# A two-layer encoder in split fp32: layer norm's PSUM bank, the first and last microseconds, the bank order of the matmuls, and inputs laid out feature-major by the host

## The chip, the cores and the metric

The kernel runs on one core of one Trainium2 chip. The metric is the device time of one execution in microseconds; lower is better. Every program shown was run several times and the median is given. A separate profiled execution gives the trace from which durations are read.

## What is computed

Two encoder layers of width 2048 over 256 tokens, with a second sequence of 256 memory tokens:

```python
def reference(x, mem, ...):
    for layer in range(2):
        h = rms_norm(x, norm_mix_g[layer])
        if layer == 0:   # conformer convolution (GLU, depthwise conv 31, layer norm, silu) beside differential attention
            x = x + mixer_conv_diff(h, ab_w_in, ..., ab_w_out)
        else:            # S5 state space, GELU, gated projection
            x = x + mixer_s5(h, ..., s5_w_val, s5_w_gate)
        x = x + memory_cross_attention(rms_norm(x, norm_xa_g[layer]), rms_norm(mem, norm_mem_g[layer]),
                                       xa_wq[layer], xa_wk[layer], xa_wv[layer], xa_wo[layer])
        x = x + conv_ffn(rms_norm(x, norm_ffn_g[layer]), ffn_w_up[layer], ffn_dw[layer], ffn_db[layer], ffn_w_down[layer])
    return rms_norm(x, final_g)
```

Everything is fp32. Nearly all the work lies in the linear layers: a [256 x 2048] activation times weights of 2048 columns and more, 5632 x 2 columns in the feed-forward (`ffn_w_up`) and back (`ffn_w_down`).

## The kernel before

**Split products.** A product of fp32 precision is made of three matmuls: weights and activations are each split into a rounded part `hi` (type fp32r) and a remainder `lo`; hi·hi, hi·lo and lo·hi are added up in PSUM. `wtile` loads 512 KB of weights into one of four `raw` buffers (queue of SP), ScalarE (ACT) casts `hi` from it (L209), VectorE (DVE) subtracts `lo` (L211); `hi` and `lo` have three buffers each.

**Two forms of the linear layer.** `lin_ws` holds weights stationary and gives the output feature-major. Per 128 rows of the contraction and for each half `c` of 256 output columns it issues one matmul of 256 columns ("low", L253: `lo` weights, `hi` activations) and one of 512 ("both", L250: `hi` weights, both parts of the activations). The halves `c` lie in two PSUM banks; a call has 64 such matmuls, 16 for each `wtile`. `lin_xs` holds activations stationary and gives the output token-major: for each 128 rows six matmuls of 512 columns, three for each token block `tb`, and the token blocks lie in two banks (L287; with `tail`, the second block's matmuls of the last weight tiles wait until the first block's are issued, L290). The accumulators of both forms come from a pool `acc` of two buffers of two banks; small PSUM tiles come from `pst`, two tags `ps` and `pt` of two banks each, taken in turn.

**Activations.** `transpose_chunk` turns 512 features of a token-major tile with 8 TensorE transposes (L156) against `ident` and evicts them as `hi` (ACT, L163) and `lo` (DVE, L164), scaled by the norm's gain. It serves the residual `X` and the memory tokens alike; the per-token factor of the norm is applied after the linear layers.

**Order.** Instructions of each engine run in the order that a scheduler of the framework sets from a simulated timeline. Beside the main line of code run generators (`self.side`): after each weight tile `background` plays some of their steps. `conv_ln` is one, with the depthwise convolution and layer norm of the conformer branch: sums over channels by matmuls with a matrix of ones into a tile `ps_mu` (mean, L518), squares `sq` (ACT, L523), sums of these into a second tile `ps_var` (L527), then `rsqrt_steps` (shift and subtract, then three Newton iterations of four DVE operations, L115 to L118), the scaling (L532), Silu (L537) and the split into `ao` (L299, L300). `ao` is the second half of the operand of the output projection `ab_w_out`; the first half, `bo`, comes from the eight attention heads, whose last step is the transpose `ps_oT` (L476).

**Memory tokens.** `mem_T(0)` stands ahead of the attention heads, `mem_T(1)` ahead of the second half of layer 0's down projection. Both transpose the memory tokens.

**Ends.** The start loads X in four chunks on SP's queue between the weight tiles of the first `lin_ws`, and small constants on POOL's queue. The end is the last down projection of layer 1 (n = 3, `tail=3`) into one accumulator, then per token block: add to X (L694), sum of squares (L696), product with the final gain (L697), the reciprocal root on one column, the scaling of four slices (L706, L708) and four output DMAs (L709).

Of the kernel before, what the change touches and what calls it, by code (L numbers as in the profile page):

```python
# [34 lines left out]
class Build:  # L35
# [43 lines left out]
    def setup(self):  # L79
# [3 lines left out]
        nc.sync.dma_start(self.X[:, :, 0:512], a["x"][0])  # L83
        nc.sync.dma_start(self.ident, a["ident"])
# [24 lines left out]
    def rsqrt_steps(self, out, v, i32, t, cost):  # L109
        nc = self.nc  # L110
        nc.vector.tensor_scalar(i32, v.bitcast(I32), 1, None, op0=ALU.logical_shift_right)
        nc.vector.tensor_scalar(i32, i32, -1, 0x5F3759DF, op0=ALU.mult, op1=ALU.add)
        y = i32.bitcast(F32)
        for it in range(3):
            nc.vector.tensor_tensor(t, y, y, op=ALU.mult)  # L115
            nc.vector.tensor_tensor(t, t, v, op=ALU.mult)
            nc.vector.tensor_scalar(t, t, -0.5, 1.5, op0=ALU.mult, op1=ALU.add)
            nc.vector.tensor_tensor(out if it == 2 else y, y, t, op=ALU.mult)  # L118
            yield cost
# [46 lines left out]

    def xslice(self, n):
# [32 lines left out]
    def wtile(self, src):  # L200
# [3 lines left out]
        dma = nc.sync.dma_start(raw, src)  # L204
# [32 lines left out]
    def lin_ws(self, w, xt):  # L237
# [5 lines left out]
        for k4 in range(4):  # L243
            hi, lo = self.wtile(w[k4])
            for kk in range(4):
                xh, _, x2 = xt(k4 * 4 + kk)
                first, last = k4 + kk == 0, k4 + kk == 6
                for c in range(2):
                    sl = slice(c * 128, c * 128 + 128)
                    both = lambda: nc.tensor.matmul(ps[:, c], lhsT=hi[:, kk, sl], rhs=x2, start=first, stop=last)  # L250
                    if first:
                        both()
                    nc.tensor.matmul(ps[:, c, 1], lhsT=lo[:, kk, sl], rhs=xh, start=False, stop=False)  # L253
                    if not first:
                        both()
# [7 lines left out]
    def lin_xs(self, w, xt, kts, ps=None, stop=True, tail=0):  # L263
# [3 lines left out]
        start = ps is None  # L267
        if start:
# [4 lines left out]
        for k2 in range(nk // KD):  # L273
            hi, lo = self.wtile(w[k2])
            for kk in range(KD):
# [3 lines left out]
                for tb in range(2):  # L279
                    sl = slice(tb * 128, tb * 128 + 128)  # L280
                    ops = [(xh, hi, first, False), (xh, lo, False, False), (xl, hi, False, last)]
                    for x, y, st, sp in ops:
# [20 lines left out]
    def mem_T(self, layer):  # L303
# [7 lines left out]
        for n in range(4):  # L311
            m = []
            for tb in range(2):
                if layer == 0:
                    m.append(mm[:, tb, n * 512 : n * 512 + 512])
                else:
                    t = self.M.tile([128, 512], F32, tag="c0", name="mst", bufs=2)
                    nc.sync.dma_start(t, a["mem"][n, :, tb])
                    m.append(t)
            if layer == 0:  # L320
                self.sumsq(m, n)
            self.mT.append(self.transpose_chunk(m, n, 6 + layer))
# [26 lines left out]
    def mixer0(self):  # L349
# [5 lines left out]
        nc.gpsimd.dma_start(cdw, a["conv_dw"])  # L355
        cv = M.tile([128, 3, 8], F32, name="cv")
        nc.gpsimd.dma_start(cv, a["conv_v"])
        nabs = M.tile([128, 2, NTOK], F32, name="nabs")
        nc.gpsimd.dma_start(nabs, a["nabs"])
        lq = M.tile([128, 4, 64], F32, name="lq")  # L360
        nc.gpsimd.dma_start(lq, a["diff_l"].partition_broadcast(128))
        sub_g = M.tile([128, 1], F32, name="sub_g")
        nc.gpsimd.dma_start(sub_g, a["subln_g"])


        lp = M.tile([128, 2, 64], F32, name="lp")
        le = M.tile([128, 2], F32, name="le")
        lam = M.tile([128, 1], F32, name="lam")
        nc.vector.tensor_tensor(lp, lq[:, 0::2, :], lq[:, 1::2, :], op=ALU.mult)
        nc.vector.tensor_reduce(le, lp, axis=AX.X, op=ALU.add)  # L370
        nc.scalar.activation(le, le, AF.Exp)
# [873 lines left out]
```

## Time and profile before

| | |
|---|---|
| runs | 2931.55, 2935.66, 2938.13 us; median 2935.66 |
| profiled execution | 2932.71 us, span 2930.9 us, mean granted TensorE clock 0.994 |
| TensorE (PE) busy | 2881.2 us, 98% of the span, 16769 matmuls |
| DVE busy | 2213.4 us, 76% |
| ACT busy | 1493.2 us, 51% |
| DMA | 674.16 MB, mean 230 GB/s |

The busy time of PE counts matmuls with modelled ends that overlap the next one, so the distance from start to start tells how fast a stream runs. Groups of instructions are named by the line of the kernel that issues them; `x128` is a count, the next numbers are busy time and the mean of one instruction in ns, and behind the bar stands the idle time of the engine just before them. A window row gives for each engine the busy time in that stretch, then the granted clock, the mean busy share of the DMA engines, and GB/s.

### The profile page before, as it was taken

What the parts mean: (1) busy time and instruction counts of PE and PEld (TensorE: products, weight loads), DVE (VectorE), ACT (ScalarE), POOL (GpSimd) and SP (SyncE); (2) the same over time, 40 slices, a digit from 0 to 9 for tenths busy, and PEclk for the clock granted to TensorE, in tenths of its full rate; (3) what the DMA queues carried; (4) which work ended last, traced back from release to release, by engine and by line L of the source; (5) the groups of instructions that cost most, each with busy time, mean ns of one, the idle gap of its engine ahead of it and who ended that gap; (6) DMA issues with size and microseconds to landing.
All of it is one profiled execution on the core that took longest, in us unless ns stands there. A gap on an engine that the chain in (4) does not pass through costs nothing. (4 is left out here: it accounts for less than half of the span.)

```text
span 2930.9 us, 44468 instructions
## 1 busy us (share of the span) xinstructions
PE 2881.2 (98%) x16769; PEld 2436.5 (83%) x16769; DVE 2213.4 (76%) x3568; ACT 1493.2 (51%) x2015; POOL 268.2 (9%) x509
## 2 busy tenths in 40 slices
PE   8999998999999999999999999999999999999998
PEld 7887887788888888888887787888888888888886
DVE  7899987877899987889855894656567776467764
ACT  5545554554455543455544554545455554345543
POOL 2100022222210012020021121000000000000000
PEclk9999999999999999999999999999999999999999
DMA  6655578988997687776697787655455555555554
GB/s 220 231 188 172 190 238 270 297 260 277 292 297 250 233 272 256 266 254 234 235 316 275 288 328 276 208 187 187 161 191 191 186 188 192 194 189 184 190 188 150
DMA packets 206023, 674.16 MB, mean 230 GB/s; under 512 B 33152, under 2 KB 35728, under 8 KB 205296
## 3 DMA queue, kind: packets, MB, share of 16 engines
q1 hardware_dynamic: 177376, 593.96, 59.1%
q0 software_dynamic: 28432, 77.36, 8.1%
q8 instruction: 131, 2.15, 0.3%
q14 instruction: 84, 0.69, 0.1%
HBM read 620.48 MB, written 61.08 MB: 233 GB/s over the span
## 5 line engine op out<-in xcount | busy, mean ns | idle before, releaser
L211 DVE TENSOR_TENSOR lo<-raw,hi 128x1024 fp32r<-128x1024 f32 x960 | 1173.6, 1224 | 546.1 <-ACT hi L209 542.6
L250 PE MATMUL ps_ws<-x,hi 128*128 128x512 f32 x4352 | 1527.8, 397 | 5.3 <-ACT hi L209 4.4
L209 ACT CAST hi<-raw 128x1024 fp32r<-128x1024 f32 x960 | 1009.0, 1051 | 1005.1 <-PE ps_xs L287 460.8
L253 PE MATMUL ps_ws<-x,lo 128*128 128x256 f32 x4352 | 1202.8, 282 | 2.9 <-DVE lo L211 2.9
L250 PEld LDWEIGHTS ps_ws<-x,hi 128*128 128x128 f32 x4352 | 809.5, 188 | 187.4 <-ACT hi L209 5.2
L253 PEld LDWEIGHTS ps_ws<-x,lo 128*128 128x128 f32 x4352 | 821.6, 189 | 20.0 <-DVE lo L211 5.0
L287 PE MATMUL ps_xs<-hi,hb 128*128 128x512 f32 x1396 | 432.0, 390 | 0.0
L287 PEld LDWEIGHTS ps_xs<-hi,hb 128*128 128x128 f32 x1396 | 262.0, 188 | 53.9
L287 PE MATMUL ps_xs<-lo,hb 128*128 128x512 f32 x698 | 272.3, 390 | 0.0
L287 PE MATMUL ps_xs<-hi,x 128*128 128x512 f32 x640 | 202.8, 395 | 0.2 <-ACT hi L209 0.2
L851 POOL DMA_DIRECT2D w1s<-d_pw x256 | 122.5, 486 | 602.2 <-PE ps_s L438 263.3
L287 PE MATMUL ps_xs<-hi,oT 128*128 128x512 f32 x512 | 160.8, 392 | 0.8 <-ACT hi L209 0.8
L287 PE MATMUL ps_xs<-hi,gT 128*128 128x512 f32 x512 | 159.3, 391 | 0.3 <-ACT hi L209 0.3
L287 PEld LDWEIGHTS ps_xs<-lo,hb 128*128 128x128 f32 x698 | 131.0, 188 | 27.0
L287 PEld LDWEIGHTS ps_xs<-hi,x 128*128 128x128 f32 x640 | 119.9, 189 | 30.3 <-issue 6.1
L287 PE MATMUL ps_xs<-lo,x 128*128 128x512 f32 x320 | 127.3, 398 | 0.0
L259 ACT COPY z<-ps_ws 128x512 f32<-128x512 f32 x88 | 51.7, 587 | 137.6 <-PE ps_ws L250 137.5
L287 PEld LDWEIGHTS ps_xs<-hi,gT 128*128 128x128 f32 x512 | 96.1, 188 | 21.3 <-issue 1.0
L656 ACT ACTIVATE c<-z,fdb,fdw 128x256 f32<-128x256 f32 x176 | 96.2, 595 | 33.0 <-DVE z L651 32.9
L287 PEld LDWEIGHTS ps_xs<-hi,oT 128*128 128x128 f32 x512 | 96.0, 188 | 20.3 <-ACT hi L209 1.0
L512 DVE SCALAR_TENSOR_TENSOR av<-hpt,cdw,av 128x256 f32<-128x256 f32 x240 | 110.7, 485 | 0.7
L260 DVE TENSOR_TENSOR z<-ps_ws,z 128x512 f32<-128x512 f32 x88 | 60.8, 691 | 55.5 <-ACT z L259 55.5
(285 smaller groups left out, 2654.6 us busy)
## 6 DMA issues: line engine op xcount, KB each, us to landing
raw<-ffn_w_up SPq DMA_DIRECT2D x352, 512.0 KB, 3.4
raw<-ffn_w_down SPq DMA_DIRECT2D x176, 512.0 KB, 4.3
raw<-ab_w_in SPq DMA_DIRECT2D x64, 512.0 KB, 3.3
raw<-xa_wv SPq DMA_DIRECT2D x64, 512.0 KB, 3.4
raw<-xa_wk SPq DMA_DIRECT2D x64, 512.0 KB, 4.5
raw<-xa_wq SPq DMA_DIRECT2D x64, 512.0 KB, 4.3
raw<-xa_wo SPq DMA_DIRECT2D x64, 512.0 KB, 3.6
w1s<-d_pw POOLq DMA_DIRECT2D x256, 64.0 KB, 6.1
```

The costliest lines, as they stand in the source:

```text
L209: nc.scalar.copy(hi, raw)
L211: ins = nc.vector.tensor_tensor(lo, raw, hi.bitcast(F32), op=ALU.subtract)
L250: both = lambda: nc.tensor.matmul(ps[:, c], lhsT=hi[:, kk, sl], rhs=x2, start=first, stop=last)
L253: nc.tensor.matmul(ps[:, c, 1], lhsT=lo[:, kk, sl], rhs=xh, start=False, stop=False)
L259: self.nc.scalar.copy(out, ps[:, :, 1])
L260: self.nc.vector.tensor_tensor(out, ps[:, :, 0], out, op=ALU.add)
L287: ins = mm()
L512: nc.vector.scalar_tensor_tensor(ac[:, ct, :], hp[:, ct, j : j + NTOK], cdw[:, ct, j : j + 1], ac[:, ct, :], op0=ALU.mult, op1=ALU.add)
L656: nc.scalar.activation(c[:, i], zt[:, i, 1 : NTOK + 1], AF.Identity, bias=fdb[:, ft : ft + 1], scale=w(1))
L851: nc.gpsimd.dma_start(pw[t * 16 : t * 16 + 16], self.d_pw[t, k * 4 : k * 4 + 4].partition_broadcast(16))
```

## The change

It joins four changes.

- Layer norm's bank: `conv_ln` puts mean and variance into the two halves of one PSUM tile `ps_ln`.
- Both ends. Start: the first weight tile goes on ACT's DMA queue, the token-major X, `ident` and the small constants are loaded on SP's queue after the first `lin_ws` in the code, and `lam` of the attention is computed after the GLU. `rsqrt_steps` scales its argument by -0.5 once and needs three DVE operations in an iteration, two where there is one column. End: the last down projection accumulates into two separate tiles `ps_e0` and `ps_e1`, and the product with the final gain becomes part of the last scaling.
- Alternating banks: `lin_ws` issues low, low, both, both over the halves `c` (in the first step both, both, low, low); `lin_xs` goes through its three products and issues each for both token blocks.
- Feature-major inputs: the host lays out `xT` and `memT`. `feature_chunk` loads 512 features of them into a buffer of the `raw` ring and splits them with 4 ACT and 4 DVE operations; it replaces `transpose_chunk` in `xt_first` and in `mem_T`. X and, in layer 0, the memory tokens are loaded token-major as well, for the residual and the sums of squares.

```diff
@@ setup
-        nc.sync.dma_start(self.X[:, :, 0:512], a["x"][0])
-        nc.sync.dma_start(self.ident, a["ident"])
+        self.begun = False
@@ rsqrt_steps
+        nc.vector.tensor_scalar(v, v, -0.5, None, op0=ALU.mult)
         for it in range(3):
-            nc.vector.tensor_tensor(t, y, y, op=ALU.mult)
-            nc.vector.tensor_tensor(t, t, v, op=ALU.mult)
-            nc.vector.tensor_scalar(t, t, -0.5, 1.5, op0=ALU.mult, op1=ALU.add)
-            nc.vector.tensor_tensor(out if it == 2 else y, y, t, op=ALU.mult)
+            if v.shape[-1] == 1:
+                nc.vector.scalar_tensor_tensor(t, y, y, v, op0=ALU.mult, op1=ALU.mult)
+            else:
+                nc.vector.tensor_tensor(t, y, y, op=ALU.mult)
+                nc.vector.tensor_tensor(t, t, v, op=ALU.mult)
+            nc.vector.scalar_tensor_tensor(out if it == 2 else y, t, 1.5, y, op0=ALU.add, op1=ALU.mult)
@@ new function
+    def feature_chunk(self, src, n, gi):
+        raw = self.W.tile([128, 1024], F32, tag="raw", name="xraw", bufs=4).rearrange("p (k t) -> p k t", k=4)
+        nc.sync.dma_start(raw, src)
+        x2 = self.S.tile([128, 4, 2, NTOK], F32R, tag=f"x2{n}", name="x2")
+        for kk in range(4):
+            g = self.gains[:, gi, n * 4 + kk : n * 4 + kk + 1]
+            nc.scalar.activation(x2[:, kk, 0], raw[:, kk], AF.Copy, scale=g)
+            nc.vector.scalar_tensor_tensor(x2[:, kk, 1], raw[:, kk], g, x2[:, kk, 0].bitcast(F32), op0=ALU.mult, op1=ALU.subtract)
@@ xt_first
-            if m:
-                self.nc.sync.dma_start(self.X[:, :, m * 512 : m * 512 + 512], self.a["x"][m])
-            self.xT.append(self.transpose_chunk(self.xslice(m), m, 0))
+            self.xT.append(self.feature_chunk(self.a["xT"][m], m, 0))
@@ wtile
-        dma = nc.sync.dma_start(raw, src)
+        dma = (nc.sync if self.begun else nc.scalar).dma_start(raw, src)
+        self.begun = True
@@ lin_ws
-                    if first:
-                        both()
-                    nc.tensor.matmul(ps[:, c, 1], lhsT=lo[:, kk, sl], rhs=xh, start=False, stop=False)
-                    if not first:
-                        both()
+                for part in (both, low) if first else (low, both):
+                    for c in range(2):
+                        part(c)
@@ lin_xs
-                for tb in range(2):
-                    ops = [(xh, hi, first, False), (xh, lo, False, False), (xl, hi, False, last)]
-                    for x, y, st, sp in ops:
+                for x, y, st, sp in [(xh, hi, first, False), (xh, lo, False, False), (xl, hi, False, last)]:
+                    for tb in range(2):
@@ mem_T
-                    t = self.M.tile([128, 512], F32, tag="c0", name="mst", bufs=2)
-                    nc.sync.dma_start(t, a["mem"][n, :, tb])
...
-            self.mT.append(self.transpose_chunk(m, n, 6 + layer))
+            self.mT.append(self.feature_chunk(a["memT"][n], n, 6 + layer))
@@ mixer0
-        nc.gpsimd.dma_start(cdw, a["conv_dw"])
...
                 pv = self.lin_ws(w[n], self.xt_first)
+                for m in range(4):
+                    nc.sync.dma_start(self.X[:, :, m * 512 : m * 512 + 512], a["x"][m])
+                nc.sync.dma_start(self.ident, a["ident"])
+                for t, v in ((cdw, a["conv_dw"]), ...):
+                    nc.sync.dma_start(t, v)
@@ conv_ln
-        pm = self.pst("ps_mu")
+        pm = self.pst("ps_ln")
+        pv = pm[:, NTOK:]
+        pm = pm[:, :NTOK]
...
-        pm = self.pst("ps_var")
         for ct in range(8):
-            nc.tensor.matmul(pm[:, :NTOK], lhsT=self.ones, rhs=sq[:, ct, :], start=ct == 0, stop=ct == 7)
+            nc.tensor.matmul(pv, lhsT=self.ones, rhs=sq[:, ct, :], start=ct == 0, stop=ct == 7)
@@ ffn
-                ps = self.lin_xs(..., tail=3 if last and n == 3 else 0)
+                ps = self.lin_xs(..., ps=[self.pst(f"ps_e{tb}", ("ps", "pt")[tb]) for tb in range(2)] if last and n == 3 else None, start=True, tail=3 if last and n == 3 else 0)
...
-            nc.vector.tensor_tensor(x, x, fg[:, 1536:2048], op=ALU.mult)
...
-                if n % 2:
+                if n == 3:
+                    nc.vector.scalar_tensor_tensor(x, x, r, fg[:, 1536:2048], op0=ALU.mult, op1=ALU.mult)
+                elif n:
                     nc.scalar.activation(x, x, AF.Copy, scale=r)
```

What that moves is seen at three places. Rows are instructions of one engine in program order; `[waits X]` names the engines or DMA queues on whose semaphores the instruction waits, `x2` repeats a row.

TensorE at the layer norm, before: the variance sums (L527) stand behind the transpose `ps_oT` of the last attention head, among the first rows of the output projection (`ps_xs`, operand `bo`).

```order
L287 MATMUL ps_xs<-hi,bo 128x512
L287 MATMUL ps_xs<-hi,bo 128x512 [waits Activation_49]
L476 MATMUL ps_oT<-ident,on 128x128 [waits Activation_49] x2
L527 MATMUL ps_var<-sq,ones 128x256 x8
L287 MATMUL ps_xs<-lo,bo 128x512 [waits DVE_49]
L287 MATMUL ps_xs<-hi,bo 128x512 x2
L287 MATMUL ps_xs<-lo,bo 128x512
```

And in the changed kernel, where the same sums are L530 (`ps_ln`):

```order
L263 MATMUL ps_ws<-x_2364,lo 128x256 x3
L262 MATMUL ps_ws<-x_2364,hi 128x512 x2
L263 MATMUL ps_ws<-x_2364,lo 128x256 x2
L530 MATMUL ps_ln<-sq,ones 128x256 [waits Activation_49]
L530 MATMUL ps_ln<-sq,ones 128x256 x3
L262 MATMUL ps_ws<-x_2364,hi 128x512 x2
L263 MATMUL ps_ws<-x_2364,lo 128x256
L530 MATMUL ps_ln<-sq,ones 128x256 [waits Activation_49]
L530 MATMUL ps_ln<-sq,ones 128x256 x3
L263 MATMUL ps_ws<-x_2364,lo 128x256
L262 MATMUL ps_ws<-x_2364,hi 128x512 x2
L478 MATMUL ps_oT<-ident,on 128x128 [waits Activation_49] x2
```

The sums moved out of the output projection into the key projection of the cross-attention (`ps_ws`, operand the memory tokens `x_2364`), ahead of a head's `ps_oT`.

ScalarE between the last up projection and the down projection of layer 0's feed-forward, before; `z` takes the output of the up projection (L259), `c` is its depthwise convolution (L656), `x_13947` a chunk of transposed memory tokens:

```order
L259 COPY z_7510<-ps_ws 128x2x256 [waits PE_49]
L209 CAST hi<-raw 128x1024 [waits DMAHW3_49,DVE_49]
L209 CAST hi<-raw 128x1024 [waits DMAHW5_49,DVE_49,PE_49]
L660 ACTIVATE c_13828<-c_13828 128x512 [waits DVE_49]
L209 CAST hi<-raw 128x1024 [waits DMAHW6_49,PE_49,Activation_49]
L656 ACTIVATE c_13932<-z_7510,fdb,fdw 128x256 [waits DVE_49]
```

And in the changed kernel, `x_13865` to `x_13887` being chunks of the memory tokens read from the `raw` ring:

```order
L177 ACTIVATE x_13865<-xraw,gains 128x256 [waits DMAHW6_49,PE_49]
L177 ACTIVATE x_13865<-xraw,gains 128x256 x3
L659 ACTIVATE c_13737<-z_7418,fdb,fdw 128x256 [waits DVE_49]
L659 ACTIVATE c_13737<-z_7418,fdb,fdw 128x256
L177 ACTIVATE x_13876<-xraw,gains 128x256 [waits DMAHW0_49,PE_49]
L177 ACTIVATE x_13876<-xraw,gains 128x256 x3
L270 COPY z_7419<-ps_ws 128x2x256 [waits PE_49]
L177 ACTIVATE x_13887<-xraw,gains 128x256 [waits DMAHW1_49]
L177 ACTIVATE x_13887<-xraw,gains 128x256 x3
L222 CAST hi<-raw 128x1024 [waits DMAHW2_49,Activation_49]
L222 CAST hi<-raw 128x1024 [waits DMAHW3_49,Activation_49]
```

The chunks stand together ahead of the first weight tile of the down projection (the two L222), and the last of them behind the copy (L270) that waits for the up projection's last matmul.

TensorE inside a `lin_ws`, before and then in the changed kernel:

```order
L253 MATMUL ps_ws<-x_216,lo 128x256 [waits DVE_49]
L250 MATMUL ps_ws<-x_216,hi 128x512 [waits Activation_49]
L253 MATMUL ps_ws<-x_216,lo 128x256
L250 MATMUL ps_ws<-x_216,hi 128x512
L253 MATMUL ps_ws<-x_216,lo 128x256
```

```order
L263 MATMUL ps_ws<-x_146,lo 128x256 [waits DVE_49]
L263 MATMUL ps_ws<-x_146,lo 128x256
L262 MATMUL ps_ws<-x_146,hi 128x512 [waits Activation_49]
L262 MATMUL ps_ws<-x_146,hi 128x512
L263 MATMUL ps_ws<-x_146,lo 128x256 x2
L262 MATMUL ps_ws<-x_146,hi 128x512 x2
```

Matmuls of one width now stand in pairs, one for each bank.

More of the change, by code (lines that the diff above doesn't have):

```diff
@@ L261, in add_parts, with lin_xs @@
         return out
[L263 removed]
+    def lin_xs(self, w, xt, kts, ps=None, stop=True, tail=0, start=False):
         nc = self.nc
[L267 to L268 removed]
+        start = start or ps is None
+        if ps is None:
             ps = self.acc.tile([128, 2, 512], F32, tag="acc", name="ps_xs")
@@ L672, in ffn @@
                 last = half == 1 and layer == 1
-                ps = self.lin_xs(a[f"ffn_w_down{layer}"][n, k0 : k0 + nk // KD], hv, list(range(nk)), tail=3 if last and n == 3 else 0)
+                ps = self.lin_xs(a[f"ffn_w_down{layer}"][n, k0 : k0 + nk // KD], hv, list(range(nk)), ps=[self.pst(f"ps_e{tb}", ("ps", "pt")[tb]) for tb in range(2)] if last and n == 3 else None, start=True, tail=3 if last and n == 3 else 0)
                 if last and n == 3:
```

48 lines of the change are left out of this document (22 added, 26 removed).

## The prediction

> **What bounds the kernel now.** I read the page's busy times, then its costliest groups, then the list of what TensorE waited for, and then windows and single instructions at each place that the change touches. A forecast of no change I take to be within 0.2% (5.9 us), about what runs of this kernel can tell apart.
>
> ```profile
> PE 2881.2 (98%) x16769; PEld 2436.5 (83%) x16769; DVE 2213.4 (76%) x3568; ACT 1493.2 (51%) x2015; POOL 268.2 (9%) x509
> ...
> L250 PE MATMUL ps_ws<-x,hi 128*128 128x512 f32 x4352 | 1527.8, 397 | 5.3 <-ACT hi L209 4.4
> L253 PE MATMUL ps_ws<-x,lo 128*128 128x256 f32 x4352 | 1202.8, 282 | 2.9 <-DVE lo L211 2.9
> ...
> L253 PEld LDWEIGHTS ps_ws<-x,lo 128*128 128x128 f32 x4352 | 821.6, 189 | 20.0 <-DVE lo L211 5.0
> ```
>
> TensorE is the bound: some 50 us of the 2930.9 are all that it stood idle. So time can come from three sources only: its waits, matmuls that go away, and the spacing of those that stay. The waits of the whole run that matter here:
>
> ```profile
> PE ps_xs L287 <- ACT ao L299: 9.9, 1, 9.9
> PE ps_xt L156 <- DMA ident<-ident: 5.2, 1, 5.2
> PE ps_ws L250 <- ACT hi L209: 4.4, 2, 4.0
> ```
>
> The first is one wait of 9.9 us for the layer-normed `ao`; the other two, 5.2 and 4.0, are the start. The windows give the start, the stretches about the long wait, and a steady stretch of `lin_ws`. The first two rows are for L250 alone.
>
> ```profile
> 0.00:30.00 30.00, 13.01 (x34) 6.86 (x35) 1.00 0.74 258
> 2200.00:2400.00 200.00, 198.63 (x569) 105.39 (x568) 1.00 0.55 187
> ...
> 480.00:492.00 12.00, 2.06 (x8) 1.27 (x7) 9.79 (x16) 6.79 (x11) 0.00 (x0) 0.67 0.81 263
> 492.00:535.00 43.00, 39.04 (x167) 31.11 (x166) 33.18 (x44) 23.28 (x37) 7.63 (x16) 0.94 0.72 233
> 450.00:480.00 30.00, 29.06 (x138) 23.76 (x136) 25.48 (x51) 12.86 (x20) 9.29 (x20) 1.00 0.97 313
> ```
>
> In the steady stretch a pair of one low and one both takes 200/569 = 0.3515 us, and 4352 pairs make 1530 us, half the run. There the clock is 1.00 and the wait lists are empty, so only the spacing itself can change.
>
> **Layer norm's bank: -11 us.** Single instructions, from the squares to the first matmul on `ao`:
>
> ```profile
> 404.88 1.06 ACT L523 ACTIVATE sq<-av 128x1024 f32<-128x1024 f32 x1
> ...
> 470.87 0.38 PE L476 MATMUL ps_oT<-ident,on 128*128 128x128 f32 x2
> 471.08 1.24 PE L527 MATMUL ps_var<-sq,ones 128*128 128x256 f32 x5
> ...
> 486.88 2.36 DVE L532 TENSOR_TENSOR av<-av,hpt 128x1024 f32<-128x1024 f32 x2
> ...
> 488.14 2.56 ACT L537 ACTIVATE av<-av,cv 128x256 f32<-128x256 f32 x5 [4.43 <-DVE av L532]
> 490.61 0.60 ACT L299 CAST ao<-av 128x512 fp32r<-128x512 f32 x1
> ...
> 491.26 0.79 PE L287 MATMUL ps_xs<-hi,ao 128*128 128x512 f32 x1 [9.94 <-ACT ao L299]
> ```
>
> The squares are ready at 405.9, yet the variance sums start at 471.08, directly behind the last head's `ps_oT`: they need a bank of `pst` that the heads go on using. From there the reciprocal root (up to 486.88, mixed with weight tiles on DVE), the scaling, Silu and `ao` take 20 us, and TensorE runs dry for 9.94. With one tile the sums need no second bank; the order of the changed kernel has them in the key projection, with well over a hundred `ws` matmuls (at 0.176 us each, over 20 us) and 96 on `bo` (0.227 each, 22 us) ahead of the first `ao`. These 20 us fit, so the wait goes: -9.9. The clock is 0.67 in the window of the wait; the matmuls behind it stand 0.43 apart instead of 0.227 (491.26, 491.85 with one more row not shown), about eight of them, another -1.7. What is late next: between 492 and 535 TensorE already lost 4 us of 43 to weight tiles that came late, and the DMA share was 0.97 just ahead. A tile that the wait gave time to arrive may now be waited for, a few us back; I take -11, and keep -4 and -18 as ends (half given back; the later waits shrink too, since their work moves).
>
> **Transposes: -7 us, and +8 for what replaces them.** A group of eight is 0.87 us in the chain:
>
> ```profile
> 1843.25 0.87 PE ps_xt L156 x8
> ```
>
> 32 transposes of `mm` and 32 of `mst` go, 64 x 0.109 = 7.0 us of pure TensorE time (those of the start are in its own term). In their place ACT and DVE work on the same number of elements, and eight chunks pass through the ring of `raw` on SP's queue, ahead of weight tiles queued behind them.
>
> ```profile
> 10.97 0.83 ACT L163 ACTIVATE x<-ps_xt,gains 128x256 fp32r<-128x256 f32 x2
> ...
> 1426.86 0.59 ACT L259 COPY z<-ps_ws 128x512 f32<-128x512 f32 x1 [1.95 <-PE ps_ws L250]
> 1427.35 1.05 ACT L209 CAST hi<-raw 128x1024 fp32r<-128x1024 f32 x1
> ...
> 1428.88 1.22 DVE L211 TENSOR_TENSOR lo<-raw,hi 128x1024 fp32r<-128x1024 f32 x1
> ```
>
> A chunk is four operations of 0.415 on ACT, 1.66 us. At layer 0's down projection ACT must, after the up projection's last matmul ends (T), do the copy (0.5), four operations (1.7) and the cast (1.05): the first matmul can start at about T + 3.5, and the next wait for `lo` adds 0.8, small ones 0.3: 4.6 us, where TensorE waited not at all before. The window above fell to 0.67 after a wait, so I add 1.4 for a slow clock: 6. At the value projection of layer 0's cross-attention two chunks stand ahead of the second weight tile: its cast starts 4.0 us into the stretch where 12 matmuls of 0.227 cover 2.7, and with `lo` that is 2 us. Sum +8; ends +2 (the ring is prefetched further than I read it) and +14 (all of it doubled where loads are late).
>
> **Start: -1 us.**
>
> ```profile
> 0.73 1.28 ACT L128 ACT_TABLE_LOAD   x1 [0.73 <-PEq L1238]
> 4.55 0.63 ACT L128 ACTIVATE junk<-X 128x512 f32<-128x512 f32 x1 [2.53 <-DMA X<-x]
> ...
> 10.02 1.04 ACT L209 CAST hi<-raw 128x1024 fp32r<-128x1024 f32 x1 [2.35 <-DMA raw<-ab_w_in]
> ...
> 11.12 0.79 PE L250 MATMUL ps_ws<-x,hi 128*128 128x512 f32 x1 [3.96 <-ACT hi L209]
> ```
>
> Before, TensorE does 34 of the 85 pairs that 30 us could hold: 18 us lost. After, no transposes and no `ident` are needed, the first weight tile comes early on its own queue, but ACT carries the start: the first chunk lands at about 5 (X did by 4.55), then follow in its order the table load 1.28 (now behind that landing), 16 chunk operations 6.6, eight squares of X at 0.75 (0.63 and its accumulator) 6.0, the two bias rows of the attention 1.1 and four casts 3.8: 23.8, and 1.2 for `lo`. The last quarter of the first `lin_ws` can start at about 25, so by 30 us stand 24 + 14 = 38 pairs, 4 more than before: -1.4, less 0.4 for 2 MB more to load. Ends -4 (squares late enough not to matter) and +3 (those 2 MB in front of weight tiles).
>
> **Tail: -4.4 us.**
>
> ```profile
> 2879.79 32.41 PE ps_xs L287 x143
> 2912.20 4.09 PE ps_xs L290 x18
> ...
> 2916.32 1.29 DVE L694 TENSOR_TENSOR X<-X,ps_xs 128x512 f32<-128x512 f32 x2 [5.85 <-PE ps_xs L290]
> ...
> 2919.23 0.27 DVE L701 TENSOR_SCALAR fv<-fv 128x1 f32<-128x1 f32 x2
> ...
> 2921.91 0.28 DVE L118 TENSOR_TENSOR fr<-rsq_i,rsq_t 128x1 f32<-128x1 f32 x2
> 2922.09 2.56 ACT L706 ACTIVATE X<-X,fr 128x512 f32<-128x512 f32 x4 [3.57 <-DVE fr L118]
> ...
> 2922.61 4.47 SPq L709 DMA_DIRECT2D out<-X x8
> ```
>
> With an accumulator each, the first block's add can start when L287 ends at 2912.2, not at 2916.3, and all its chain and four of the eight output DMAs lie beside the last 18 matmuls. The second block keeps its add and square (2916.3 to 2918.3), loses the gain product between them and the root (0.7) and one of the two interleaved chains: from L701 to the end of L118 15 operation steps at 0.195 become 10, -1.0. Its four DMAs are issued in half of 4.47: -2.2. With 0.5 for ACT's four scalings instead of eight shared: -4.4. Ends -3 and -5.5.
>
> **Alternating banks: -10 us.** In the trace, boundaries between two `lin_ws` calls show widths in pairs, as the new order has them:
>
> ```profile
> 2304.07 0.62 PE L250 MATMUL ps_ws<-x,hi 128*128 128x512 f32 x2
> 2304.53 0.28 PE L253 MATMUL ps_ws<-x,lo 128*128 128x256 f32 x1
> 2304.64 0.40 PE L250 MATMUL ps_ws<-x,hi 128*128 128x512 f32 x1
> 2304.87 0.40 PE L253 MATMUL ps_ws<-x,lo 128*128 128x256 f32 x2
> 2305.11 0.40 PE L250 MATMUL ps_ws<-x,hi 128*128 128x512 f32 x1
> ```
>
> From 2304.07 to 2305.11 are three pairs, 1.04 us against 3 x 0.3515 = 1.055. With one pair of boths and one of lows in them, that is a gain of 15 ns, in rows rounded to 10; the mean over the starts at all such boundaries is 0.699 for a group of four against 0.703, and 2176 groups give -10. Bounds: nothing at the least, and at the most the two lows at their 0.12 (2304.87) and the boths at the 0.2266 of the rows of `lin_xs` above: 2 x (0.12 + 0.2266) = 0.693, -22. `lin_xs` gains nothing: its 143 matmuls with a bank change every third take 32.41/143 = 0.2266 each, and the 18 that stay in one bank 4.09/18 = 0.2272.
>
> The pages speak against this part. The Trainium skill, "TensorE: Matmul & The Clock Gate", section "Back-to-back issue gap", gives the distance of warm matmuls as N/2.4 + 2.5 ns, with no word of banks; an estimate by it is 216 + 109 = 325 ns for a pair, where the trace has 351.5, and the alternation would be worth nothing. Its section on psum-queue depth-cycling tells of a kernel in which moving through banks made the clock oscillate; the steady window here has 1.00 though `lin_ws` before changes its bank after every second matmul, so the trace does not agree.
>
> **The sum.** -11 - 7 + 8 - 1 - 4.4 - 10 = -25.4 on the profiled execution's 2932.7, 2907. The median of the runs stands 3 us above that execution, so 2910 on the median of 2935.66.
>
> **The rivals.**
> - The alternation gives nothing. For it: both streams of `lin_xs` stand at 227 whether the bank changes or not; against it: the 4 ns in the mean at the boundaries. Without -10: 2920.
> - The spacing reaches its bound or passes it. For it: half of 0.2266 for a low makes a pair 0.340, and the trace has 0.3515; those 11.5 ns, 50 us over 4352 pairs, are the price of some change, of bank or of width, and the new order halves the changes of width. -22 to -35, with -27 in the middle, instead of -10: 2893.
> - The wait moves: layer norm's chain is early but weight tiles are not, and the chunks in the `raw` ring double their cost. For it: the share 0.97 of the DMA engines at 450 to 480. -4 for -11, +14 for +8: 2923, or 2928 with half of the alternation's gain.
> - Slower: two lows in a row need two loads of stationary weights in a row, and a load takes 189 ns (L253, PEld) where a low takes 0.12. If the second load can't begin before the first low does, it sticks out by 0.189 - 0.12 = 0.069 in each group: 2176 x 0.069 = +150, 2920 + 150 = 3070. It decides from a group of 0.710 on, 7 ns above before, where it eats the 15 us of the other parts. Against it: 2304.87 shows two lows within 0.24 us.
>
> **How the numbers follow.** Forecast 0.45; nothing from the alternation 0.27; the bound or more 0.15; the moved wait 0.08; slower by loads, or by something in the order that I don't see, 0.05. The likeliest gives 2910. The range runs from 2884, past the bound's 2893 with the best start and tail, to 2928, past the moved wait; about 0.08 lies below and 0.1 above. Faster by more than 0.2% are the first three and some of the fourth: 0.89; within 0.2% the rest of it and mixtures, 0.06; slower 0.05.
>
> **What would show it.** In the profile after: no wait of `ps_xs` for `ao`, and L530 ahead of 420 us; waits for `hi` or `lo` of some 5 us at the first down projection of layer 0; the last L297 and L300 matmuls within 10 us of the end; a steady window with 571 to 573 pairs in 200 us if the alternation gives 10, 569 if nothing, 577 at its bound. Wrong would be: 531 pairs or fewer there, or new waits of more than 15 us together.

## The result, and the profile after

Before 2934.53 us (median of 4 runs, 2931.55 to 2938.13), after 2917.39 (2910.70 to 2921.53): ratio 0.9939, 95% interval 0.9917 to 0.9961, or 17 us less. The profiled execution after took 2910.7 us, the fastest of the runs shown; it is 22 us below the one before, so 5 of its 22 are a lucky run. A second series gave 2916.48 and 0.9942 (0.9929 to 0.9955); one of the nine runs of the kernel before beside it took 3554 us at a clock of 0.75 and is left out of that ratio.

The page of the changed kernel, the two halves of `lin_ws`, and what TensorE waited for in the whole run:

```profile
PE 2859.3 (98%) x16673; PEld 2415.2 (83%) x16673; DVE 2204.1 (76%) x3524; ACT 1492.9 (51%) x2015; POOL 265.2 (9%) x504
...
L262 PE MATMUL ps_ws<-x,hi 128*128 128x512 f32 x4352 | 1352.4, 396 | 9.9 <-ACT hi L222 9.9
...
L263 PE MATMUL ps_ws<-x,lo 128*128 128x256 f32 x4352 | 846.0, 280 | 8.9 <-DVE lo L224 8.6
```

```profile
PE ps_ws L262 <- ACT hi L222: 9.9, 1, 9.9
PE ps_ws L263 <- DVE lo L224: 8.6, 5, 5.3
PE ps_xs L297 <- ACT hi L222: 7.8, 7, 3.2
PE ps_xs L297 <- DVE lo L224: 7.3, 12, 1.3
```

The wait of 9.9 for `ao` is gone (the 9.9 for `hi` is now the whole start). In its place stand one of 5.3 (start), one of 3.2 (layer 0's down projection) and more short ones for `hi` and `lo` than before. All waits of TensorE together are 38.8 us, where before had 34.9, so the change does not win by waiting less in sum. As an estimate from this case's numbers, 96 transposes fewer at 0.109 (10.5 us), the shorter tail (4.4) and the denser stream (7, told below) come to 21.9, about the 22 of the two profiles. The longer waits take 3.9 of that back, and a mean granted clock of 0.996, where before had 0.994, gives about as much again.

The busy time of the two groups fell by 175 and 357 us, but no time of that size was saved: modelled ends of neighbours on one line overlap, and they are counted once when the two stand together. For the speed of a stream only starts count.

To see at which place time is won or lost, I take from both traces the moment when TensorE has started the same amount of the linear layers' matmuls (a both or a `lin_xs` matmul counts 2 units, a low 1) and subtract. A negative number is a lead over before, in us.

| place in before's trace, us | after | ws_only | ln_only | tail_only |
|---|---|---|---|---|
| 102, end of the start | +1.3 | -0.7 | -1.1 | -0.3 |
| 453, ahead of the output projection | +4.1 | +0.6 | +3.6 | -0.3 |
| 560, behind it | -12.4 | -5.0 | -5.5 | -9.8 |
| 750, layer 0's feed-forward begins | -8.5 | +5.1 | -0.6 | -8.2 |
| 1417, its last up projection | -11.4 | +2.2 | -1.9 | -9.2 |
| 1527, S5 | -7.9 | +2.1 | -1.9 | -9.2 |
| 2166, layer 1's feed-forward begins | -12.4 | +0.8 | -2.0 | -7.1 |
| 2916, last matmul | -17.6 | -4.5 | -2.0 | -7.2 |
| end of the span | -22.0 | -4.5 | -1.9 | -11.8 |

The last three columns are kernels with one part of the change each, told below. Each column is one execution. Two of the changed kernel (`after` and the later run after_again) differ by some 2 us up to the row of 1527 and by 5 to 6 from 1600 us on: at the last matmul the second one is ahead by 11.9, not 17.6, and at the end of the span by 16.3. Differences of that size between two columns show nothing by themselves.

The next rows of the changed kernel show the new waits: at the start, where the `lo` of the third weight tile is late, and at layer 0's down projection (instructions of TensorE, then of ScalarE).

```profile
17.41 0.63 PE L262 MATMUL ps_ws<-x,hi 128*128 128x512 f32 x2
23.30 0.80 PE L263 MATMUL ps_ws<-x,lo 128*128 128x256 f32 x2 [5.27 <-DVE lo L224]
23.90 1.05 PE L262 MATMUL ps_ws<-x,hi 128*128 128x512 f32 x2
```

```profile
1414.47 0.63 PE L262 MATMUL ps_ws<-x,hi 128*128 128x512 f32 x2
1418.31 1.22 PE L297 MATMUL ps_xs<-hi,hb 128*128 128x512 f32 x2 [3.21 <-ACT hi L222]
1420.12 1.22 PE L297 MATMUL ps_xs<-lo,hb 128*128 128x512 f32 x2 [0.59 <-DVE lo L224]
```

```profile
1415.14 0.59 ACT L270 COPY z<-ps_ws 128x512 f32<-128x512 f32 x1 [1.08 <-PE ps_ws L262]
1415.62 1.70 ACT L177 ACTIVATE x<-xraw,gains 128x256 fp32r<-128x256 f32 x4
1417.23 1.98 ACT L222 CAST hi<-raw 128x1024 fp32r<-128x1024 f32 x2
```

After each of these waits two matmuls of 512 columns take 1.05 to 1.22 where 0.63 is usual, and the granted clock is 0.50 from 23 to 28 us and from 1418 to 1424. The Trainium skill, "TensorE: Matmul & The Clock Gate", section "Part 1: The HAM clock gate", says that an idle window of about 3.4 us halves the clock. The trace agrees in so far as the clock is at half when the idle gaps of 5.27 and 3.21 us end. But gaps well below 3.4 us can do it too, and the length of the gap alone does not decide it: after the wait of 1.82 us for `qT` that ends at 614.2 the clock is 0.50 too, from 615.2 to 618.5, while after one of 2.52 that ends at 1555.7 it is 1.00.

### The profile page after: what moved, and what is told of

It is laid out like the page before. It is cut to its first block, busy times and chain, and to the rows that moved or that the text cites. A ratio compares the mean times of both kernels' runs of the same rounds, so it can differ in the third digit from the quotient of the medians.

```text
span 2908.9 us, 44257 instructions
## 1 busy us (share of the span) xinstructions
PE 2859.3 (98%) x16673; PEld 2415.2 (83%) x16673; DVE 2204.1 (76%) x3524; ACT 1492.9 (51%) x2015; POOL 265.2 (9%) x504
## 5 line engine op out<-in xcount | busy, mean ns | idle before, releaser
L222 ACT CAST hi<-raw 128x1024 fp32r<-128x1024 f32 x960 | 1008.2, 1051 | 981.7 <-PE ps_xs L297 431.2
L262 PE MATMUL ps_ws<-x,hi 128*128 128x512 f32 x4352 | 1352.4, 396 | 9.9 <-ACT hi L222 9.9
L263 PEld LDWEIGHTS ps_ws<-x,lo 128*128 128x128 f32 x4352 | 795.1, 188 | 191.0 <-DVE lo L224 13.7
L263 PE MATMUL ps_ws<-x,lo 128*128 128x256 f32 x4352 | 846.0, 280 | 8.9 <-DVE lo L224 8.6
L262 PEld LDWEIGHTS ps_ws<-x,hi 128*128 128x128 f32 x4352 | 675.2, 189 | 23.4 <-ACT hi L222 10.1
L297 PE MATMUL ps_xs<-hi,hb 128*128 128x512 f32 x1328 | 358.2, 391 | 3.2 <-ACT hi L222 3.2
L297 PE MATMUL ps_xs<-lo,hb 128*128 128x512 f32 x664 | 206.3, 392 | 0.8 <-DVE lo L224 0.8
L297 PE MATMUL ps_xs<-hi,x 128*128 128x512 f32 x640 | 177.2, 394 | 0.8 <-ACT hi L222 0.8
L297 PE MATMUL ps_xs<-hi,oT 128*128 128x512 f32 x512 | 141.1, 392 | 0.8 <-ACT hi L222 0.8
L297 PE MATMUL ps_xs<-hi,gT 128*128 128x512 f32 x512 | 138.1, 391 | 0.3 <-ACT hi L222 0.3
L270 ACT COPY z<-ps_ws 128x512 f32<-128x512 f32 x88 | 51.7, 587 | 144.8 <-PE ps_ws L262 144.8
L297 PE MATMUL ps_xs<-lo,x 128*128 128x512 f32 x320 | 100.7, 394 | 1.8 <-DVE lo L224 1.8
```

The costliest lines, as they stand in the source:

```text
L222: nc.scalar.copy(hi, raw)
L262: both = lambda c: nc.tensor.matmul(ps[:, c], lhsT=hi[:, kk, sl[c]], rhs=x2, start=first, stop=last)
L263: low = lambda c: nc.tensor.matmul(ps[:, c, 1], lhsT=lo[:, kk, sl[c]], rhs=xh, start=False, stop=False)
L270: self.nc.scalar.copy(out, ps[:, :, 1])
L297: ins = mm()
```

## The experiments

**Bank or width?** In the change both alternate differently: banks change at each matmul instead of at every second, widths at every second instead of each. Four kernels, each the kernel before with another order in `lin_ws` alone (loops shortened; the first and last steps of a call differ a little).

```diff
 # ws_only: the change's loop
+ for part in (both, low) if first else (low, both):
+     for c in range(2): part(c)
 # ws_same_bank: the same widths, one bank at a time; two steps i of the contraction together
+ for c in range(2):
+     for part in (low, both):
+         for i in range(2): part(i)
 # ws_cross: banks alternate, widths too (the four steps i of a weight tile)
+ for c in range(2):
+     for i in mid: low(i, c), both(i, 1 - c)
 # ws_fours: four lows, then four boths, banks alternating
+ for part in (low, both):
+     for i in range(2):
+         for c in range(2): part(i, c)
```

> The kernel before with the new order of lin_ws alone (low, low, both, both over the two banks). In the changed kernel the steady window 2200 to 2400 us held 1149 matmuls, a pair of low and both in 348.1 ns, against 1137 and 351.8 before. If the order does that: 1149 +- 2 matmuls in the same window here and 4352 x 3.7 ns = 16 us less in all, about 2918 on 2934.5. Rival: the order gives nothing and the denser window comes from the other parts: 1137, and no change of the time.

> The kernel before with widths in pairs as in the change, but of the same bank: low, low, both, both of one half c for two steps of the contraction, then of the other; the bank changes twice in 8 matmuls (before 4, in the change 8), the width 4 times (before 8, in the change 4). If fewer changes of width save the time: 348 ns a pair (1149 matmuls in 200 us), as in the change. If the alternation of banks saves it: 352 to 354 (1130 to 1137).

> The kernel before with banks alternating at nearly every matmul, but widths too: low of one bank, both of the other, over the four steps of a weight tile, then with the banks swapped (the first and last step of a call stay as in the change). If fewer changes of width save the time: 351 to 352 ns a pair (1137 to 1139 matmuls in 200 us, for the few steps that differ). If the alternation of banks saves it: 348 (1149).

> The kernel before with four lows and then four boths (two steps of the contraction, banks alternating at every matmul): the width changes twice in 8. If changes of width cost what 8 against 4 of them in 8 showed, half of 3.7 ns a pair more is saved: 346.2 (1155 matmuls in 200 us). If the alternation of banks is it: 348 (1149), as in the change.

The steady window 2200 to 2400 us (behind the length of the window stands PE's busy time, with its number of matmuls in brackets) of before, ws_only, ws_same_bank, ws_cross and ws_fours:

```profile
2200.00:2400.00 200.00, 200.00 (x1137) 173.77 (x1136) 147.37 (x198) 113.01 (x145) 0.00 (x0) 1.00 0.55 187
```
```profile
2200.00:2400.00 200.00, 200.00 (x1148) 174.53 (x1148) 148.72 (x198) 113.37 (x146) 0.00 (x0) 1.00 0.57 189
```
```profile
2200.00:2400.00 200.00, 200.00 (x1149) 174.61 (x1148) 148.68 (x198) 111.84 (x144) 0.00 (x0) 1.00 0.58 189
```
```profile
2200.00:2400.00 200.00, 200.00 (x1136) 173.68 (x1135) 147.13 (x196) 111.96 (x144) 0.00 (x0) 1.00 0.56 187
```
```profile
2200.00:2400.00 200.00, 200.00 (x1144) 175.10 (x1143) 148.66 (x198) 112.92 (x145) 0.00 (x0) 1.00 0.58 189
```

In this window the banks do nothing: widths in pairs in one bank are as dense as the change (1149, the changed kernel has 1149), and alternating banks with alternating widths as before (1136). So it is the order of the widths. But fewer changes are not better without end: fours (1144) lie between. In the traces from 2000 to 2400 us the mean distance from start to start of two lows is 115 in a pair and 119 in the middle of a four, a both behind a low costs 235.6 in the old order and 233.1 in pairs. Why runs of four lows are slower is open; each low needs a load, and that loads pace a longer run is only an argument.

In time ws_only is 2926.8 against 2934.0, ratio 0.9978 (0.9969 to 0.9987): 7 us, not the 16 that I expected from that window (one execution each: ws_same_bank 2923.2, ws_cross 2934.6, ws_fours 2934.5). The window was not typical of before. From one low to the next, where nothing else stands between and no wait, a pair takes in its trace 349.0 ns on average (690 to 1000 us), 350.5 (1200 to 1400) and 352.5 (2000 to 2400), while ws_only has 348.9, 348.9 and 349.0. Over the whole run it is 351.2 against 349.0, which makes 9.6 us for 4352 pairs, just above the 4 to 9 that were measured.

The profile of ws_only is only 4.5 us shorter than that of before, for a second reason. In the table it loses 10 us between 560 and 750 us: TensorE waits 1.9 us for `qT` and more for weight tiles, and the clock falls to 0.91 in 620 to 640 and 640 to 660. ws_same_bank is 2.6 ahead at 560 and 2.2 at 750, and its single execution is the shortest of the four. Whether the loss belongs to the order of ws_only or to that execution is open.

**Layer norm's bank alone, and the ends alone.** ln_only is the kernel before with `ps_ln`; tail_only the kernel before with the new `rsqrt_steps`, the two accumulators and the folded gain.

```diff
 # ln_only
+        pm = self.pst("ps_ln")
+        pv = pm[:, NTOK:]
+        pm = pm[:, :NTOK]
 # tail_only
+        nc.vector.tensor_scalar(v, v, -0.5, None, op0=ALU.mult)   # and three operations an iteration
+        ps = self.lin_xs(..., ps=[self.pst("ps_e0", "ps"), self.pst("ps_e1", "pt")], start=True, tail=3)
```

> The kernel before with mean and variance in one PSUM tile, nothing else. The prediction has -11 us for it, ends -4 and -18: the wait of 9.9 us for ao goes, and the slow clock behind it. In the changed kernel the lead grew by 12.5 us between the stretches at 453 and 743 us. If that is the bank alone: no wait for ao, 10 to 13 us faster. Rival: VectorE or late loads of this stage bound it, and the wait comes back as several for lo and hi: 3 to 6 us faster.

> The kernel before with the shorter reciprocal root, the two accumulators of the last projection and the gain folded into the last scaling, nothing else. Prediction -4.4 us (ends -3 and -5.5); in the changed kernel the span ended 10.7 us after the start of the last matmul, against 15.0 before. If the tail is a matter of its own: the same 4.3 us here. Rival: the shorter root also shortens the waits at the norms: 5 to 7 us.

(The diff of tail_only is shortened; the folded gain is not shown.) Measured: ln_only 2931.70 against 2932.37, ratio 0.9994 (0.9986 to 1.0003), less than the rival had; tail_only 2920.92, ratio 0.9962 (0.9950 to 0.9975), 11 us, more than its rival had. Waits of TensorE from 350 to 560 us, before, ln_only and tail_only:

```profile
PE ps_xs L287 <- ACT ao L299: 9.9, 1, 9.9
PE ps_xs L287 <- DVE lo L211: 3.6, 5, 1.5
PE ps_xs L287 <- ACT hi L209: 1.3, 1, 1.3
```
```profile
PE ps_xs L287 <- DVE lo L211: 5.9, 6, 1.5
PE ps_xs L287 <- ACT hi L209: 2.2, 2, 1.2
PE ps_ws L253 <- DVE lo L211: 1.2, 2, 0.8
PE ps_xs L287 <- ACT bo L477: 0.6, 1, 0.6
```
```profile
PE ps_xs L290 <- ACT hi L212: 3.9, 3, 2.8
PE ps_xs L290 <- DVE lo L214: 2.0, 4, 1.0
PE ps_xs L290 <- ACT ao L302: 1.3, 1, 1.3
PE ps_xs L290 <- DVE ao L303: 0.7, 1, 0.7
```

The variance sums and the last transposes of the heads in ln_only, then in tail_only (number of instructions, shortest, median and longest in ns, first and last start in us):

```profile
L528 PE MATMUL ps_ln<-sq,ones x16: 377/379/380, 406.6 to 410.3; 128*128 128x256 f32 x16
L476 PE MATMUL ps_oT<-ident,on x16: 270/271/330, 305.2 to 480.1; 128*128 128x128 f32 x16
```
```profile
L530 PE MATMUL ps_var<-sq,ones x16: 379/380/381, 456.0 to 459.2; 128*128 128x256 f32 x16
L479 PE MATMUL ps_oT<-ident,on x16: 270/271/274, 306.2 to 455.9; 128*128 128x128 f32 x16
```

In ln_only the sums start at 406.6 instead of 471.1 and no wait for `ao` is left, as predicted. But 5 us of waits, nearly all for weight tiles, take its place. One cause is seen in DVE, which now does part of the work earlier. The windows 420 to 460 us of before and ln_only (DVE's busy time comes third among the engines, behind PE and PEld):

```profile
420.00:460.00 40.00, 39.95 (x227) 34.30 (x225) 32.94 (x57) 16.59 (x24) 11.44 (x24) 1.00 0.92 296
```
```profile
420.00:460.00 40.00, 38.77 (x217) 32.97 (x216) 38.76 (x70) 23.89 (x35) 11.44 (x24) 1.00 0.94 296
```

DVE goes from 32.9 to 38.8 of 40 us, TensorE loses its first 1.2 there, and the last head's `ps_oT` comes at 480.1 instead of 471.0. Late loads have a share as well: two waits of 0.95 and 0.76 us at 499 are for tiles that landed only at 497.4 and 499.1. How the 5 us divide between the two is not shown. At 560 us the kernel is 5.5 ahead, and by 655 it has given back all but 0.5: 2.8 us of new waits (the longest 1.5, for `qT`, the output of the query projection), a clock of 0.91 in 620 to 640, and in that stretch attention products in another order. That last piece I have not taken apart.

tail_only keeps the second bank; its variance sums still stand directly behind the last `ps_oT`, at 456.0, but that is 15 us earlier, while the output projection begins at the same time (453.1 before, 452.8 here). So 83 matmuls on `bo` now stand between the sums and the first on `ao`, where before had 29, and the wait for `ao` falls from 9.9 to 1.3. Before the end, the code of tail_only differs by nothing but the reciprocal root, which the norms, the eight heads and the layer norm call: fewer DVE operations, in chains that the next step waits for. So the shorter root alone takes most of this wait away and wins time, and the freer bank alone takes it away and wins almost none. Whether the last head comes earlier by DVE's load, by the shorter chains or by the order that the scheduler makes of them, no run here tells, and no run undoes one of the two in the changed kernel. At the end of the span tail_only gains 4.6, the predicted 4.4.

**The start.** Both kernels are the changed kernel with X loaded later. x_late puts X's loads and the small constants behind the fourth weight tile (`with self.tc.issue_after(self.last_dma)`); x_spread puts one chunk of X behind each weight tile of the second `lin_ws` and the squares behind that call (shown, shortened):

```diff
+        if self.late:                       # in wtile
+            with self.tc.issue_after(dma.ins):
+                for t, v in self.late.pop(0):
+                    nc.sync.dma_start(t, v)
```

> The changed kernel with the loads of the token-major X and of the small constants put behind the fourth weight tile of the first lin_ws. In the changed kernel the third feature chunk landed at 16.6 us behind 2 MB of X, ACT took X's eight squares (12.3 to 18.2) ahead of it, and TensorE waited 5.7 us at 17.6. If X's loads and squares are that wait, it goes and the time falls by 4 to 5 us. Rival: ACT's own chain of chunks and casts bounds the start anyway, or the fifth weight tile, now behind X, is as late: 0 to 1 us.

> The changed kernel with X's four loads spread one by one behind the four weight tiles of the second lin_ws, and the squares and the norm behind that call. Moving all four behind the fourth tile moved the wait of 5.7 us from 17.6 to 24.0 us. If the wait is for 2 MB that share the DMA engines with the weights (the share was 0.83 in the first 30 us), spreading them over tiles that leave room (0.57 in a steady stretch) takes most of it away: 4 to 6 us faster than the changed kernel. Rival: ACT's chunks and casts bound the start: 0 to 1 us.

Measured: x_late 2916.99, the same as the changed kernel beside it (2916.48); x_spread 2910.73, ratio to before 0.9921 (0.9909 to 0.9934), some 6 us below the changed kernel. Waits of TensorE in the first microseconds, in the changed kernel, x_late and x_spread:

```profile
PE ps_ws L262 <- ACT hi L222: 9.9, 1, 9.9
PE ps_ws L263 <- DVE lo L224: 5.3, 1, 5.3
```
```profile
PE ps_ws L263 <- ACT hi L223: 15.0, 2, 10.1
PE ps_ws L264 <- DVE lo L225: 0.6, 2, 0.4
```
```profile
PE ps_ws L267 <- ACT hi L227: 10.3, 1, 10.3
PE ps_ws L268 <- DVE lo L229: 0.2, 1, 0.2
```

In x_late the wait of 5 us is only moved, to the fifth weight tile; in x_spread it is gone. ACT's squares of X moved along with the loads in both, but they are the smaller part. In the changed kernel the third chunk, issued at 9.5, lands at 16.6 behind X, and the third weight tile at 18.7; in x_late the same chunk, issued at 9.6, lands at 12.8. The squares hold up the cast of that tile by 1.1 us more, to 19.8. In x_late the fifth tile lands at 27.9 and its cast starts at 28.2. So this wait is mostly set by the bytes that stand ahead of a tile, and the 2 MB of X do no harm once they share the time of running matmuls.

**Memory tokens.** mem0_tr takes layer 0's transposes back; mem1_late puts `feature_chunk` n of layer 1 behind down projection n.

```diff
 # mem1_late: no chunks ahead, one in each turn of the loop over the four down projections of layer 0
-                self.mem_T(1)
+                self.mT = []
...
                     self.s5_in(n)
+                    self.mT.append(self.feature_chunk(a["memT"][n], n, 7))
```

> The changed kernel with layer 0's memory tokens transposed on TensorE again (32 matmuls, 3.5 us), the chunks of layer 1 as in the change. If the chunks in the raw ring cost what the prediction says (2 us of waits at the value projection), the transposes are dearer: 1.5 us slower. In the changed kernel four waits between 250 and 258 us add up to over 3 us with a slower stream; if these come from the chunks, this version is 0 to 3 us faster.

> The changed kernel with layer 1's memory chunks each put behind one of the four down projections of layer 0 instead of ahead of them all. In the changed kernel TensorE waited 3.3 us for hi at 1414.7, then 1.0 for lo, and lost 1 to 2 more to a slow clock. If ACT's chunks ahead of the first weight tile are the cause, these waits go and the time falls by 5 to 7 us. Rival: the transition between the two projections needs that time anyway, or the chunks stop a weight tile elsewhere: 0 to 2 us.

> The changed kernel once more, for its time beside the next three, and a second profile. Its first profiled execution took 2910.7 us, the median of four 2917.4. If the waits behind the layer norm (2.1 us at 612, weight tiles late) depend on how the loads fall, this profile differs from the first there and nowhere else; if not, the waits agree within 1 us each.

Measured: mem0_tr 2923.05, 6.6 us slower than after_again (2916.48); mem1_late 2908.01, 8.5 faster, ratio to before 0.9916 (0.9902 to 0.9930). mem1_late has no wait at all between 1400 and 1440 us, as expected. In its profiled execution, the slowest of its five, a wait of 2.9 for a weight tile stands at 1463 instead, and from 1417 to 1527 us it loses 3.8 us of its lead, where the two profiles of the changed kernel lose 3.6 and 4.6. So no trace shows the 8.5 us; they rest on the medians alone, and the runs overlap (2906.5 to 2916.3 against 2910.6 to 2919.9).

In mem0_tr the waits about 255 us go too, but the transposes' time and two waits of 1.2 and 1.1 for `lo` at 426 to 430 cost more; its lead at 750 us is 4.0, where the two profiles of the changed kernel have 8.5 and 7.4. In the stage from 200 to 560 us a wait that goes tends to be made up by a later one. after_again's profile, with the same program, has the waits of the first at the same places within some 0.6 us, but for one of 1.2 more in the output projection (at 547), one for `qT` of 0.8 instead of 1.8 with more short ones behind it, and one of 1.9 more at S5 (at 1557). These are the parts that vary with how the loads fall.

**Both repairs.** both_better joins x_spread and mem1_late.

> The changed kernel with X's loads spread as in x_spread and layer 1's memory chunks behind the four down projections as in mem1_late (which was 8.5 us faster than the changed kernel). If the two are independent: 12 to 14 us faster than the changed kernel, about 2903. If start time is taken back in the stage of layer 0 that waits for loads, only the 8 of mem1_late stay: about 2908.

Measured: 2908.34, ratio to before 0.9917 (0.9903 to 0.9930). It equals mem1_late alone; the start's 6 us are not added. In its profile the lead over after_again is some 4 us at 43 us and 1.9 at 743, so in this execution part of the start's gain goes in layer 0. But x_spread, in which TensorE has the same instructions in the same order up to 1407 us, still leads after_again by 6.3 at 743; so that loss is how one execution fell. Why the medians do not add up is open. It and mem1_late are the fastest kernels here, 8 to 9 us below the change.

## Why the prediction was right, and where its steps failed

The total was right: forecast 2910 with a range of 2884 to 2928, measured 2917.4; faster, as forecast, by 17 us where the sum had 25. That it came so near is in part luck: the layer norm's bank alone gave 10 us less than its term, and the shorter reciprocal root gave 7 us more than its own, which the prediction had not looked for. The terms one by one:

- **Layer norm's bank, -11.** The step failed. The mechanism was read rightly (the sums wait for a bank behind the heads, and the bank frees them), but its price was taken to be the wait. Alone it is worth -0.7 us (+1 to -4): my rival "the wait moves" came true there. I had blamed late loads; ln_only shows these too, but also DVE, 38.8 of 40 us busy. The changed kernel does gain 12.6 us between 453 and 750 (10.8 in its second profile), as much as forecast, though the bank alone does not give it.
- **Ends, -4.4.** The tail itself was right: 4.4 in the changed kernel (22.0 less 17.6 in the table) and 4.6 in tail_only. What I left out is that `rsqrt_steps` is called in the heads and the layer norm too; I costed its new form at the end alone. tail_only gains another 7 us by it, in the stage where I had the wait for `ao`. That this is what the changed kernel gains there is argued from the two kernels with one part each, not shown by taking the root out of the changed kernel.
- **Transposes and chunks, -7 + 8.** At layer 0's down projection the forecast was 4.6 us of waits and 1.4 of slow clock; measured 3.21 + 0.59 of waits, and 6.5 us of lead lost between 1417 and 1430, as forecast (7.0 in the second profile). The value projection had 2.6 us of waits where I had 2. But undoing layer 0's chunks cost 6.6 us, not the 1.5 expected; the sum of single stalls and matmuls missed that waits in that stage exchange for each other.
- **Start, -1.** The step failed, by little: measured +1.3, with 28 boths started by 30 us where I had 38. I saw the squares and the 2 MB and counted ACT's time for them, yet not that the third chunk and the third weight tile would land behind X; the wait of 5.3 us is mostly that, as x_late and x_spread show.
- **Alternating banks, -10.** Measured -7 (-4 to -9). The size was near, but the mechanism was wrong: I called it banks, and it is the order of the widths. My evidence, pairs of widths at the boundaries of `lin_ws`, was in truth evidence on widths (and its 4 ns over 2176 groups are 8.7 us, which I had as 10). The rival that put the spacing on changes "of bank or of width" came nearest to the reason, with too large a price, 22 to 35 us. The formula of the Trainium skill, "Back-to-back issue gap" in "TensorE: Matmul & The Clock Gate", has the number of columns alone and no term for banks; its section calls it the gap of a single matmul and says that in a stream the weight loads set the spacing too. That banks do not enter agrees with ws_same_bank and ws_cross. That columns alone count does not hold for this stream, since the same two widths, with as many loads, take 351.8 or 348 ns a pair in that window by their order.
- **`lin_xs`, 0.** No experiment undid it alone; in the changed kernel's last projection 65 matmuls, most with the banks in turn, take 14.73 us, 0.2266 each, and 18 in one bank 4.09, or 0.2272 each, the same as the prediction had from before.

```profile
2879.83 14.73 PE ps_e L297 x65
2894.56 4.09 PE ps_e L300 x18
```

Of what the prediction named as signs, most came: no wait for `ao`, the sums ahead of 420 us, waits of some 5 us at layer 0's down projection, and 574 pairs in the steady window, one more than it had for a gain of 10. The last matmul starts 10.7 us ahead of the end, where it had 10. New waits came close to the 15 us that it would have called wrong: those of `lin_xs` for `hi` and `lo` rose from 7.9 to 15.1 us, those of `lin_ws` for `lo` from 2.9 to 8.6, and 1.8 for `qT` is new. The rival with loads that serialise did not come, but ws_fours leaves room for something of the kind in a longer run of lows.

## What to carry to other kernels

A wait of 10 us need not be 10 us of gain: ask which engine's work and which loads the wait gave room to, and whether there is room where the work moves to. When a helper gets cheaper, look up every place that calls it, first of all in the stage where its engine is nearly full. And here loads that nobody needed soon did least harm one by one behind the tiles of a running stream, not ahead of it or in a block. Last, one profile is one execution: two of the same program differed by 5.7 us at the last matmul.

## What was not expected of the hardware

The order of the widths sets the pace of a dense matmul stream: lows of 256 and boths of 512 columns, each with its own stationary load, take 351.8 ns a pair when they alternate and 348 in twos, with four and four between (349.7), at a granted clock of 1.00 and whatever the bank. In the old order the pace also drifts with the place in the run, from 349.0 to 352.5 ns, while in twos it stays at 348.9 to 349.0; what makes it drift is open.

And a short wait can cost more than itself: in the changed kernel 1.82 us without a matmul were followed by 3.3 us at a granted clock of 0.50. A longer wait of 2.52 was not, so what decides it is not the length of the wait alone.
